# Loading two experts' input weights in 8 KB rows, with tokens gathered in the matching channel order

## The chip, the cores and the metric

The program runs on one core of a Trainium2 chip. The metric is the device time of one execution in microseconds (us); the runs of the kernel before took 2385.02, 2388.09 and 2391.01 us, a median of 2388.09. A core has a matrix engine (PE, whose weight loads are shown as PEld), a vector engine (DVE), a scalar engine (ACT), a GpSimd engine (POOL) and a sync engine (SP). Here SP issues nearly all transfers from HBM, and 16 DMA engines carry them.

## The reference

One layer of a hybrid backbone works on 512 latent tokens and 256 context tokens of 2048 channels: modulated norm, one input projection, three branches (convolution, neighbourhood attention, a gated recurrence), an output projection with a gated residual, and then a mixture of 32 experts, which is where the change lies. Everything is float32.

```
h  = modulated RMSNorm of the residual stream         # 512 x 2048
pg = softmax(h @ w_rg);  grp = argmax                 # one of 4 groups
le = (h @ w_re) of that group; the two best of 8 experts, weights p_exp
for each expert e and its tokens x:
    y = (silu(x @ w1[e]) * (x @ w3[e])) @ w2[e]       # 2048 -> 512 -> 2048
out = residual + gate * sum of the weighted y;  final RMSNorm
```

For each expert `w1` and `w3` are 2048 x 512 and `w2` is 512 x 2048, 4 MB each. The 32 experts' weights are 403 MB in all, out of 589 MB that the kernel reads.

## The kernel before, in words

The order of all instructions is written by hand; engines run their own queues in that order. The input projection takes the first half, then comes the output projection (until about 1300 us), the routing of tokens (to about 1312 us), and the experts, two at a time, in 16 passes that I number as pairs 0 to 15.

Each expert has 64 slots for tokens. A pair uses the two halves of PE's columns: expert `e` in columns 0 to 63, `e + 1` in 64 to 127, so two matmuls run side by side. For the products with `w1` and `w3` (`expert_pair`, matmul at L1359) the gathered tokens `hs[k]` (128 channels by 256 slots) are the stationary side, and the weights of the same 128 channels (128 x 512) are the moving side; 16 contraction steps `k` are summed. Then come the activation (L1370, L1386), a transpose (L1391), the product with `w2` in four runs of 512 columns (`down`, L1403), the scaling by slot weights (`scaled`, L1410), a split into high and low parts (L124, L125) and a product with a one-hot matrix that returns the slots to their tokens (`combine`, L1338), which DVE adds to the residual (L1340).

Weights come in tiles of 1 MB. `add` (L1034) cuts `w1` and `w3` so that one tile holds two contraction steps of both experts: partition p holds channel 128 k + p, so each piece that a partition receives is one weight row of 512 floats, 2 KB. `load_weights` (L1059) issues two transfers of 512 KB for a tile, one for each expert, as far ahead as there are places: six in a pool of their own (`NW`), one in the experts' pool, and eight former homes of other data, of which five are given back during the first two pairs (`until`). Ten stay. `next_w` (L1076) hands out the next tile when its first matmul is written, and returns the place of the one before it. A tile lasts four of the paired matmuls. There are 24 tiles to a pair: 8 of `w1`, 8 of `w3`, 8 of `w2`.

Four experts' tokens are gathered at a time by products with a one-hot matrix (`gather`, L1267). It has 16 steps: four runs of 512 channels, for each four blocks of 128 tokens. For a step, `token_parts` (L1139) makes the high part of 128 tokens by 512 channels on ACT (L1149, a cast) and the low part on DVE (L1150, a subtraction), and eight matmuls (L1291) follow. Two steps' parts are kept at a time, so a step's parts are made after the matmuls of the step two before it. After each fourth step DVE scales four channel tiles with the modulation `A2` and the norm (L1307), and ACT adds `B2` (L1308). The gather for the next four experts goes on beside the odd pairs: three steps each beside the first two quarters of `w3`, two each beside the others, one after them, four beside the `w2` products, and one in the next pair (`STEPS`). The first gather comes before and beside pair 0; its first three low parts are made on POOL, beside the routing on DVE.

During the output projection `constant` (L1012) works out the constant part of the router's logits on DVE and PE, in ticks 14 and 15 of 64.

Of the kernel before, what the change touches and what calls it, by code (L numbers as in the profile page):

```python
# [8 lines left out]
F32 = mybir.dt.float32  # L9
# [3 lines left out]
AF = mybir.ActivationFunctionType  # L13
# [19 lines left out]
NSTART = 6                      # units of the input projection that go on beside the start  # L33
LEAD = 2
SUMS = (3, 6, 9)                # steps of a modulation run at which the sums of the run before go on
BUDGET, ATTN, MOST = 0.7, 1.0, 3  # what a tick has room for on the vector engine
NW = 6                          # weight tiles in their own pool
# [9 lines left out]
def hybrid_block_kernel(ctx: ExitStack, tc: tile.TileContext, I, out):  # L47
# [13 lines left out]
    # ---------------------------------------------------------------- constants  # L61
# [21 lines left out]
    sel = vec[:, 300:302]           # rows 32 g + {0, 1}  # L83
    strips = vec[:, 302:306]        # rows 32 g
    sc = work.tile([P, KT, 2], F32, name="sc")
    nc.scalar.activation(sc, c_in, AF.Silu)
    mods = const.tile([P, 6, KT, 2], F32, name="mods")   # A1, B1 of both streams; ga1, B2, A2, ga2
    warm = const.tile([P, 1], F32, name="warm")

    def table(f):  # L90
        """has the scalar engine's table ready before it is needed"""
        nc.scalar.activation(warm, ones[:, 0:1], f)
# [3 lines left out]
    def rsqrt_newton(dst, v, r):  # L96
        """one Newton step from r towards dst = v ** -0.5; v is lost"""
# [4 lines left out]
    # ------------------------------------------------------------------ tiles  # L102
# [25 lines left out]
    # ------------------------------------------------------------------ start: norm and modulation  # L128
    cs = work.tile([P, KT, 32], F32, name="cs", tag="bias", bufs=2)   # zero-padded stationaries
# [9 lines left out]
    # weights in the order of their use: of the modulation, and of the first units  # L139
# [59 lines left out]
    def modulated(k):  # L199
        """the modulated tokens of a channel tile, in two parts"""  # L200
# [5 lines left out]
    def product(po, h, l, mh_, ml_, first, last):  # L206
        """high x high, high x low and low x high parts"""
# [26 lines left out]
    # three steps for a channel tile: its modulation's rows; its tokens; its products  # L234
# [23 lines left out]
    def context():  # L258
        """its norm and modulation"""
# [38 lines left out]
    # ------------------------------------------------- masks  # L298
# [11 lines left out]
    # ------------------------------------------------- work that goes on beside the projections  # L310
    mix = {}
    taps = deque()        # single instructions of the depthwise convolution
    stages = deque()      # generators of the branches, run one after the other
    mod_ops = deque()

    def step(n=1):
        """the next steps of the branches; returns what they leave for the end of the tick"""
# [14 lines left out]
    # ---- the rest of the modulation: weighted rows summed on the vector engine, partitions on the tensor engine  # L332
# [53 lines left out]
    # ---- convolution module, channel-major  # L386
# [55 lines left out]
    # ---- gated linear recurrence, channel-major, chunks of 128  # L442
# [14 lines left out]
    def context_key(d, fc, kc):  # L457
        """context keys, each decayed to the end of the context, in place of the decays' tile"""
# [23 lines left out]
    def hgrn(h, z, vals, q, g):  # L482
        iv, ivc = vals
        near = (1, 0)                                     # half of a block that holds t; the other holds s
        pp = [z[0][0], z[1][0]]                           # decay from the start of its block to a query
        ks = [z[0][1], z[1][1]]
        st = [t2("st0"), t2("st1")]                       # decay from a key to the end of its block
# [30 lines left out]
        def products(b, keys, queries, other=0):  # L518
            """of keys with queries of the same half of a chunk, or of the other one"""
# [120 lines left out]
    def by_unit(t):  # L640
        """natural token order seen as (column unit of 8, row, column)"""
        return t.rearrange("p (r u c) -> p u r c", r=ROWS, c=8)
# [1029 lines left out]
```

## Time and profile before

| what | value |
|---|---|
| median of three runs | 2388.09 us (2385.02 to 2391.01) |
| profiled execution: span, first to last instruction | 2378.7 us |
| what lies around the span (median less span) | 9.4 us |
| PE busy | 2248.1 us, 95% |
| DVE, ACT, POOL busy | 1259.8, 692.0, 268.8 us |
| moved by DMA | 600.81 MB, of it 317232 packets on SP's queue |
| packets of 8 KB and more | 162 of 321234 |

The page gives no time of its own for the profiled execution beside its span; the median is 9.4 us above the span, which is taken as constant. A busy time of PE includes the modelled ends of matmuls, so a PE that is busy 95% of the time may still be waiting a little in each matmul: start times are the better measure, and most readings below use them. In rows of a timeline the first number is the start in us from the span's start, the second how long the merged instructions took, then engine, line, operation, what is written and read, shape and count, and in brackets the idle time before and what ended it.

### The profile page before, as it was taken

The page shows a single profiled execution, that of the slowest core. Times are in us where ns is not written, and L with a number is a line of the kernel's source. Part 1 is how long each engine was busy: PE and PEld are TensorE (multiplying, and loading weights), DVE is VectorE, ACT ScalarE, POOL GpSimd, SP SyncE. Part 2 cuts the span into 40 slices and gives each one's busy share as a digit, 9 for nine tenths or more (in the row PEclk, how much of TensorE's full clock was granted, in tenths as well). Part 3 has the DMA queues.
Part 4 walks back from the last instruction along what each step waited for, and adds up shares of the span by engine and source line. Part 5 has one row for each costly group of instructions (what it writes and reads, how often), then busy time and mean ns, then how long its engine had stood idle before and what let it go on. Part 6 is the DMA issues. An engine that isn't in the chain of part 4 may idle for free. (4 is left out here: it accounts for less than half of the span.)

```text
span 2378.7 us, 32438 instructions
## 1 busy us (share of the span) xinstructions
PE 2248.1 (95%) x12145; PEld 1416.7 (60%) x12145; DVE 1259.8 (53%) x2204; ACT 692.0 (29%) x1382; POOL 268.8 (11%) x320
## 2 busy tenths in 40 slices
PE   6998999989899999999999999999999999999996
PEld 2456877778777878787777544444534444444433
DVE  4348898898876666434323344443524333434424
ACT  4235223323244453445343321121203121211202
POOL 0006133152421111212000000000000000000000
PEclk9999999999899999999999999999999999999998
DMA  8875434434464555322645799999999999999997
GB/s 304 275 254 170 133 104 132 140 99 135 148 184 150 160 164 158 105 70 63 208 140 199 245 361 336 387 386 387 386 386 386 387 386 386 386 384 387 384 387 264
DMA packets 321234, 600.81 MB, mean 253 GB/s; under 512 B 25392, under 2 KB 35376, under 8 KB 321072
## 3 DMA queue, kind: packets, MB, share of 16 engines
q1 hardware_dynamic: 317232, 593.44, 71.8%
q0 software_dynamic: 3840, 5.25, 1.0%
q8 instruction: 97, 1.59, 0.3%
q14 instruction: 65, 0.53, 0.1%
HBM read 589.15 MB, written 4.19 MB: 249 GB/s over the span
## 5 line engine op out<-in xcount | busy, mean ns | idle before, releaser
L210 PE MATMUL p<-xh,wl 128*128 128x512 f32 (+1 forms) x1184 | 421.2, 356 | 39.1 <-DVE wl L125 35.6
L208 PE MATMUL p<-xh,wh 128*128 128x512 f32 (+1 forms) x1184 | 434.0, 367 | 2.6 <-ACT wh L124 2.2
L1359 PE MATMUL held<-w,hg 128*64 128x512 f32 x1848 | 428.7, 597 | 3.7 <-DMA w<-w 3.0
L209 PE MATMUL p<-xl,wh 128*128 128x512 f32 (+1 forms) x1184 | 418.4, 353 | 0.0
L1359 PEld LDWEIGHTS held<-w,hg 128*64 128x64 f32 x1848 | 129.8, 136 | 251.1 <-issue 211.2
L125 DVE TENSOR_TENSOR wl<-w,wh 128x512 fp32r<-128x512 f32 x216 | 173.7, 804 | 197.6 <-ACT wh L124 192.7
L210 PEld LDWEIGHTS p<-xh,wl 128*128 128x128 f32 x1184 | 225.0, 190 | 83.9 <-DVE wl L125 48.1
L208 PEld LDWEIGHTS p<-xh,wh 128*128 128x128 f32 x1184 | 225.2, 190 | 43.2 <-issue 8.0
L209 PEld LDWEIGHTS p<-xl,wh 128*128 128x128 f32 x1184 | 225.4, 190 | 31.7 <-issue 1.4
L124 ACT CAST wh<-w 128x512 fp32r<-128x512 f32 x216 | 133.8, 620 | 375.4 <-PE p L209 286.6
L1403 PE MATMUL held<-w,at 128*64 128x512 f32 (+1 forms) x944 | 211.9, 591 | 10.9 <-ACT at L1393 10.9
L351 DVE SCALAR_TENSOR_TENSOR m_acc<-w_ada,sc,m_acc 128x512 f32<-128x512 f32 x240 | 213.2, 889 | 13.8 <-DMA w_ada<-w_ada 10.5
L1340 DVE TENSOR_TENSOR xf<-pc,xf 128x512 f32<-128x512 f32 (+1 forms) x244 | 149.6, 675 | 50.6 <-PE pc L1338 50.5
L1150 DVE TENSOR_TENSOR parts<-xr,parts 128x512 fp32r<-128x512 f32 x112 | 76.9, 692 | 170.7 <-ACT parts L1149 170.7
L1291 PEld LDWEIGHTS held<-oh,parts 128*128 128x128 f32 x896 | 112.2, 188 | 66.9 <-issue 46.9
L1291 PE MATMUL held<-oh,parts 128*128 128x256 f32 x896 | 129.3, 290 | 14.2 <-ACT hg L1308 10.3
L1403 PEld LDWEIGHTS held<-w,at 128*64 128x64 f32 x944 | 62.7, 136 | 127.2 <-issue 107.8
L1149 ACT CAST parts<-xr 128x512 fp32r<-128x512 f32 x112 | 68.7, 620 | 170.2 <-PE held L1291 169.4
L124 ACT CAST wh<-ys 128x512 fp32r<-128x512 f32 x60 | 37.2, 620 | 255.2 <-DVE ys L1410 147.7
L1338 PE MATMUL pc<-wh,oht 128*128 128x512 f32 (+1 forms) x260 | 105.8, 408 | 0.0
L208 PE MATMUL po<-mx,wh 128*128 128x512 f32 x256 | 103.0, 402 | 1.1 <-ACT mx L977 0.7
L1338 PE MATMUL pc<-wl,oht 128*128 128x512 f32 (+1 forms) x260 | 101.7, 392 | 0.1
(349 smaller groups left out, 2852.9 us busy)
## 6 DMA issues: line engine op xcount, KB each, us to landing
w<-w SPq DMA_DIRECT2D x692, 512.0 KB
w_ada<-w_ada SPq DMA_DIRECT2D x384, 256.0 KB
w<-w_in SPq DMA_DIRECT2D x184, 256.0 KB
wm<-w SPq DMA_DIRECT2D x74, 512.0 KB
w<-w_out SPq DMA_DIRECT2D x64, 256.0 KB
w_st<-w_st SPq DMA_DIRECT2D x32, 192.0 KB
x<-xT SPq DMA_DIRECT2D x16, 256.0 KB
xt<-xT SPq DMA_DIRECT2D x16, 256.0 KB
```

The costliest lines, as they stand in the source:

```text
L124: nc.scalar.copy(wh, w)
L125: nc.vector.tensor_sub(wl, w, wh.bitcast(F32))
L208: nc.tensor.matmul(po, h, mh_, start=first, stop=False)
L209: nc.tensor.matmul(po, h, ml_, start=False, stop=False)
L210: nc.tensor.matmul(po, l, mh_, start=False, stop=last)
L351: nc.vector.scalar_tensor_tensor(accs[j], loads.popleft(), sc[:, kt, 0:1], accs[j], op0=ALU.mult, op1=ALU.add)
L1150: engine.tensor_tensor(l, x_, h.bitcast(F32), op=ALU.subtract)
L1291: nc.tensor.matmul(pg[i], y[:, cc(i)], oh[:, t], start=t == 0 and m == 0 and i % 2 == 0, stop=t == 3 and m == 1 and i % 2 == 1)
L1338: nc.tensor.matmul(pc[:, 0:n], oht[:, cc(t)], y[:, 0:n], start=m == 0, stop=m == 1)
L1340: nc.vector.tensor_tensor(x_, pc[:, 0:n], x[:, t, o:o + n], op=ALU.add)
L1359: nc.tensor.matmul(acc[64 * j:64 * j + 64], hs[k][:, sl + 64 * j:sl + 64 * j + 64], w[:, j, k % 2], start=k == 0, stop=k == KT - 1, tile_p ...
L1403: nc.tensor.matmul(pd[64 * j:64 * j + 64, 0:n], at[:, 128 * f + 64 * j:128 * f + 64 * j + 64], w[:, j, f - f0], start=f == 0, stop=f == 3, ...
```

## The change: what it does

`w1` and `w3` are cut another way. A tile holds one expert's 512 channels 512 c to 512 c + 511, and partition p gets the four neighbouring channels 512 c + 4 p + i, i = 0 to 3. These are 8 KB in one run of HBM. One transfer of 1 MB brings a tile. A quarter `c` of the contraction now takes two tiles at once, one of each expert, which `next_w(2)` hands out together. `w2` is left as it was.

A contraction step must then have tokens' channels 512 c + 4 q + i on partition q. `token_parts` reads the residual in that order, every fourth float, and writes the parts contiguously as before. The modulation vectors `A2` and `B2` are needed in the same order (`mod2`): 16 small matmuls with every fourth column of the identity, and one copy, do that in tick 15 of the output projection. Comments are taken out of the file as well, which moves line numbers only.

```diff
+    mod2 = const.tile([P, 2, KT], F32, name="mod2")
...
             nc.vector.tensor_tensor(cl, pcn[:, 0:NL], br, op=ALU.add)
+            pq = bank("pq")
+            for m in range(4):
+                for i in range(4):
+                    nc.tensor.matmul(pq[32 * m:32 * m + 32, 0:2 * KT].rearrange("p (w g i) -> p w g i", w=2, i=4)[:, :, :, i],
+                                     ident[:, i::4], mods[:, 3:5, m::4, 0], start=True, stop=True, tile_position=(0, 32 * m))
+            nc.vector.tensor_copy(mod2, pq[:, 0:2 * KT].rearrange("p (w k) -> p w k", w=2))
...
+    def add_run(name, e, c):
+        wseq.append((0, 0, I[name][e, 512 * c:512 * c + 512].rearrange("(p k) n -> p k n", p=P)))
...
-            for k in range(0, KT, 2):
-                add(name, e, k, 2, 0, 512)
+            for c in range(4):
+                for j in range(2):
+                    add_run(name, e + j, c)
...
-                w = rows(w, nk, c)
-                for j in range(2):
-                    nc.sync.dma_start(w[:, j], v[:, j])
+                if nk:
+                    w = rows(w, nk, c)
+                    for j in range(2):
+                        nc.sync.dma_start(w[:, j], v[:, j])
+                else:
+                    nc.sync.dma_start(w, v)
...
-        x_ = xr[:, t, 512 * c:512 * c + 512]
+        x_ = xr[:, t, 512 * c:512 * c + 512].rearrange("p (q i) -> p i q", i=4)
...
-        nc.scalar.copy(h, x_)
-        engine.tensor_tensor(l, x_, h.bitcast(F32), op=ALU.subtract)
+        h4, l4 = (y.rearrange("p (i q) -> p i q", i=4) for y in (h, l))
+        nc.scalar.copy(h4, x_)
+        engine.tensor_tensor(l4, x_, h4.bitcast(F32), op=ALU.subtract)
...
-                    nc.vector.scalar_tensor_tensor(h, pg[i], A2[:, k:k + 1], norm, op0=ALU.mult, op1=ALU.mult)
-                    nc.scalar.activation(h, h, AF.Identity, bias=B2[:, k:k + 1])
+                    nc.vector.scalar_tensor_tensor(h, pg[i], mod2[:, 1, k:k + 1], norm, op0=ALU.mult, op1=ALU.mult)
+                    nc.scalar.activation(h, h, AF.Identity, bias=mod2[:, 0, k:k + 1])
...
+                ws = next_w(2)
                 for k in range(4 * c, 4 * c + 4):
-                    if k % 2 == 0:
-                        w = next_w()
                     for j in range(2):
-                        nc.tensor.matmul(acc[64 * j:64 * j + 64], hs[k][:, sl + 64 * j:sl + 64 * j + 64], w[:, j, k % 2],
+                        nc.tensor.matmul(acc[64 * j:64 * j + 64], hs[k][:, sl + 64 * j:sl + 64 * j + 64], ws[j][:, k % 4],
                                          start=k == 0, stop=k == KT - 1, tile_position=(0, 64 * j))
```

## Rows read from the trace of the kernel before

**Rows 1.** The page: its first line, and what the DMA engines moved in each of 40 equal slices of the span (59.5 us each).

```profile
span 2378.7 us, 32438 instructions
...
GB/s 304 275 254 170 133 104 132 140 99 135 148 184 150 160 164 158 105 70 63 208 140 199 245 361 336 387 386 387 386 386 386 387 386 386 386 384 387 384 387 264
```

**Rows 2.** The table by stretches, for 1500 to 2300 us: stretch, its length, then busy time (and count) of PE, PEld, DVE, ACT and POOL, PE's granted clock, the DMA engines' mean busy share, GB/s.

```profile
1500.00:2300.00 800.00, 770.51 (x3727) 356.47 (x3725) 325.82 (x586) 147.39 (x273) 0.00 (x0) 1.00 1.05 386
```

**Rows 3.** Who waited for whom, from 1319 to 2352 us: who, for whom, us in total, times, longest.

```profile
PEld held L1359 <- DMA w<-w: 32.8, 71, 1.2
```

**Rows 4.** PE's timeline: the matmuls of L1376, which stand between a pair's `w1` and `w3` products, of the odd pairs 1, 3, 5, 7, 9, 11, 13 and 15.

```profile
1398.33 0.86 PE L1376 MATMUL pa<-aux,oh 128*128 128x33 f32 x6
...
1526.83 0.74 PE L1376 MATMUL pa<-aux,oh 128*128 128x33 f32 x5
...
1655.67 0.74 PE L1376 MATMUL pa<-aux,oh 128*128 128x33 f32 x5
...
1787.11 0.74 PE L1376 MATMUL pa<-aux,oh 128*128 128x33 f32 x5
...
1917.07 0.74 PE L1376 MATMUL pa<-aux,oh 128*128 128x33 f32 x5
...
2048.62 0.86 PE L1376 MATMUL pa<-aux,oh 128*128 128x33 f32 x6
...
2179.98 0.74 PE L1376 MATMUL pa<-aux,oh 128*128 128x33 f32 x5
...
2309.84 0.86 PE L1376 MATMUL pa<-aux,oh 128*128 128x33 f32 x6
```

**Rows 5.** PE's timeline: L1376 of pair 14 and the transposes L1391 that follow its `w3` products; a stretch of the `w3` products of pair 15, and the transposes that follow them.

```profile
2255.65 0.74 PE L1376 MATMUL pa<-aux,oh 128*128 128x33 f32 x5
...
2271.48 0.65 PE L1391 MATMUL pt<-cf,act 128*128 128x128 f32 x4 [0.86 <-DVE act L1386]
...
2318.82 2.43 PE L1359 MATMUL held<-w,hg 128*64 128x512 f32 x8 [0.28 <-DMA w<-w]
...
2332.45 0.65 PE L1391 MATMUL pt<-cf,act 128*128 128x128 f32 x4 [0.86 <-DVE act L1386]
```

**Rows 6.** The DMA view, SP's queue: packets, MB, and the time that they took as a share of 16 engines' time; first for 1500 to 2300 us (weights, packets of 2 KB), then for 2371 to 2378.7 us (the last stores of the output, in packets of 4 KB).

```profile
q1 hardware_dynamic: 159884, 308.22, 104.4%
...
q1 hardware_dynamic: 578, 2.10, 67.7%
```

**Rows 7.** The timeline of the gather beside pair 7: its step 2 (first three rows), steps 10 and 11 up to the transposes L1391 (next five), and the `w2` products' first quarter (last four).

```profile
1793.65 0.62 ACT L1149 CAST parts<-xr 128x512 fp32r<-128x512 f32 x1 [4.82 <-PE held L1291]
1794.31 0.69 DVE L1150 TENSOR_TENSOR parts<-xr,parts 128x512 fp32r<-128x512 f32 x1 [2.65 <-ACT parts L1149]
...
1795.05 1.10 PE L1291 MATMUL held<-oh,parts 128*128 128x256 f32 x7 [0.26 <-DVE parts L1150]
...
1816.81 0.62 ACT L1149 CAST parts<-xr 128x512 fp32r<-128x512 f32 x1 [1.29 <-PE held L1291]
1817.47 0.69 DVE L1150 TENSOR_TENSOR parts<-xr,parts 128x512 fp32r<-128x512 f32 x1 [2.52 <-ACT parts L1149]
1817.76 0.62 ACT L1149 CAST parts<-xr 128x512 fp32r<-128x512 f32 x1 [0.33 <-PE held L1291]
...
1819.02 0.68 DVE L1386 TENSOR_TENSOR act<-held,act 128x512 f32<-128x512 f32 x1
...
1819.76 0.66 PE L1391 MATMUL pt<-cf,act 128*128 128x128 f32 x4 [0.45 <-DVE act L1386]
...
1825.81 0.62 ACT L1149 CAST parts<-xr 128x512 fp32r<-128x512 f32 x1 [4.78 <-PE held L1291]
...
1827.08 1.65 DVE L1307 SCALAR_TENSOR_TENSOR hg<-held,mods,norm 128x256 f32<-128x256 f32 x4
...
1828.64 0.74 DVE L1410 SCALAR_TENSOR_TENSOR ys<-held,tw,ga2b 128x512 f32<-128x512 f32 x1
...
1830.82 0.50 PE L1338 MATMUL pc<-wl,oht 128*128 128x512 f32 x1
```

**Rows 8.** DVE's timeline: the reduction L1014, which reads 576 floats at a step of 144 bytes; a reduction of 128 neighbouring floats (L1197); two products of 256 floats each at a step of 8 bytes (L501). Then, from the view of line L1271, products of 256 floats of which one side is read in order: shortest, median and longest time in ns.

```profile
1146.43 1.20 DVE L1014 TENSOR_REDUCE ws<-wr 128x36 f32<-128x576 f32 x1
...
1303.72 0.29 DVE L1197 TENSOR_REDUCE me<-lg 128x16 f32<-128x128 f32 x1
...
285.55 0.76 DVE L501 TENSOR_TENSOR qq<-hq,f 128x256 f32<-128x256 f32 x2
...
L1271 DVE TENSOR_TENSOR oh<-iota,place x32: 415/419/426, 1311.5 to 2182.5; 128x256 fp32r<-128x256 f32 x32
```

**Rows 9.** The timeline of the routing: POOL's three low parts, and two of DVE's instructions beside them.

```profile
1304.23 2.64 POOL L1150 TENSOR_TENSOR wl<-xr,wh 128x512 fp32r<-128x512 f32 x2 [48.33 <-ACT wh L1149]
...
1304.45 1.28 DVE L1203 SCALAR_TENSOR_TENSOR w<-lg,rev 128x144 f32<-128x144 f32 x1
...
1306.81 1.32 POOL L1150 TENSOR_TENSOR part<-xr,part 128x512 fp32r<-128x512 f32 x1
1306.94 1.23 DVE L1209 TENSOR_TENSOR gh<-w,gm 128x16 f32<-128x16 f32 x1
```

**Rows 10.** PE's timeline in the input projection: a small product of four columns (two records to a matmul), and the matmul after it.

```profile
681.18 0.28 PE L364 MATMUL pm<-vec,rows 128*128 128x4 f32 x2
681.32 0.48 PE L208 MATMUL p<-xh,wh 128*128 128x512 f32 x1
```

More of the change, by code (lines that the diff above doesn't have):

```diff
@@ L1070, in load_weights, with next_w @@
                     w = four(at, "w")
-                w = rows(w, nk, c)
-                for j in range(2):
-                    nc.sync.dma_start(w[:, j], v[:, j])
+                if nk:
[4 more added lines that the diff above has]
+                    nc.sync.dma_start(w, v)
                 wtiles.append((w, at))
-    def next_w():
+    def next_w(n=1):
         places.extend(used)
@@ L1080, in next_w @@
         load_weights()
-        w, at = wtiles.popleft()
-        used.append(at)
-        return w
+        ws = []
+        for _ in range(n):
+            w, at = wtiles.popleft()
+            used.append(at)
+            ws.append(w)
+        return ws if n > 1 else ws[0]
     def beside_out(i, n):
```

## The prediction

> **What bounds the kernel now.** I read the page first, to see which stages are full of what [rows 1]: transfers run far below their best for most of the kernel, and at 384 to 387 GB/s without a dip from about 1490 us to 2320 us. That is the experts' stage, the only one whose loads change. The table by stretches says that both candidates are full there: PE busy 770.5 of 800 us at its full granted clock, DMA engines at 1.05, 386 GB/s [rows 2]. So busy shares do not tell which of the two sets the end, and I went to the waits [rows 3]: PE's weight loads for the `w1` and `w3` products waited 32.8 us for weights, in 71 waits. Part of this overlaps running matmuls, so I measured the loss by start times.
>
> The matmuls of L1376 stand at the same place of each odd pair; from one to the next lies the same work, four experts [rows 4]. The seven distances are 128.50, 128.84, 131.44, 129.96, 131.55, 131.36 and 129.86 us. The shortest is PE's own pace; the excess of the others over it is 0.34 + 2.94 + 1.46 + 3.05 + 2.86 + 1.36 = 12.0 us. After the last of them come the `w3` products of pair 15: 2332.45 - 2309.84 = 22.61 us, where those of pair 14, with the same work, took 2271.48 - 2255.65 = 15.83; the bracket in between names the wait for `w` [rows 5]. That is 6.8 us more. The transfers' own pace explains it: a tile of 1 MB at 386 GB/s takes 2.72 us, 48 tiles 130.4 us, against 128.5 us for PE. The stage is bound by transfers by a hair: 12.0 + 6.8 = 18.8 us in all is what PE loses to them, and no speed of loading can win more.
>
> **The change part by part.**
>
> *The packets.* In 1500 to 2300 us SP's queue took 1.044 x 16 x 800 = 13,363 us of engine time for 308.22 MB, 88.8 ns for 2 KB; at the end, in 4 KB packets, 0.677 x 16 x 7.7 = 83.4 us for 2.10 MB, 163 ns for 4 KB, that is 81 ns for 2 KB [rows 6]. Those are stores, and the trace has no bulk load in larger packets, so the gain has two ends: nothing, or, when a part per packet (88.8 + 88.8 - 163 = 15 ns) is paid once instead of four times, 12% of the time of `w1` and `w3`. I take what the 4 KB row itself shows, 8%: 2.49 us a tile. A loss from larger packets is excluded by nothing but this row. What decides is only whether transfers fall below PE's pace: 32 x + 16 x 2.72 = 128.5 gives x = 2.66 us, so 2% is enough. At 2.49 the four experts take 123.2 us and the 18.8 us go.
>
> *Two tiles at a time.* A quarter now needs two tiles before its second matmul and returns them together, 3.44 us later. Of ten places two are in use, eight hold a lead. The greatest demand is the end: from L1376 of pair 14 to the end of `w3` of pair 15, 54.2 + 15.8 = 70 us [rows 4, 5], 32 tiles that arrive in 24 x 2.49 + 8 x 2.72 = 81.5 us: 11.5 us short, 4.6 tiles of eight. It fits, so I cost this at nothing while transfers are quicker; if they are not, each of the last quarters starts up to a tile later, and the cover is gone (rival 2). SP issues 256 fewer transfers; it has nothing else to do here.
>
> *Tokens read at a step of 16 bytes.* `token_parts` reads as many floats as before, so a gain is excluded. DVE at a step of 8 bytes shows no price: two instructions of 256 floats in 0.76 us, where in-order ones take 0.42 each. At 144 bytes it shows one: L1014 took 1.20 us for 576 floats, and from 0.29 us for 128 and 1.05 ns a float ((0.69 - 0.42) us over 256, L1150 against L1271) it would be 0.76 [rows 7, 8]. The excess is 0.76 ns a float, 0.39 us for 512. Sixteen bytes lies between, much nearer to 8; but the two rows differ in that at 144 bytes no two floats lie together, and at 16 bytes with runs of one the reads are of that sort too. I take 0.39 us on DVE (ends 0 and 0.39). ACT shows no such read; its ends are the same, and I take the middle, 0.2.
>
> Where it is paid [rows 7]: at step 2 PE waits already for the parts, made 0.62 + 0.69 us after the step before the last; the chain grows by 0.59 and PE with it. At steps 10 and 11, DVE's second low part now ends near 1819.8 and L1386, queued behind it, near 1820.5 instead of 1819.70; the transposes wait for it: 0.8 us. In the first `w2` quarter L1307 and L1410 stand behind the part on DVE, and the split and the return to tokens, with no room left at 1830.82, behind them: 0.59. The other steps' parts are ready microseconds ahead. Together 2.0 us per gather, seven gathers: 13.9 us (9.7 with a free ACT, 17.9 with 0.39 there, 0 with both free).
>
> *The first gather.* POOL's three low parts take 1.3 us each, and DVE's products in the routing do not end before them: L1203 took 1.28 us and L1209 1.23 for 144 and 16 floats [rows 9]. The routing leads to the first matmul of the experts, so what POOL loses, PE loses: 0 to 3 x 0.39 = 1.2 us by DVE's price; I take 1.2. [...]
>
> *`mod2`.* Sixteen small matmuls on PE in the output projection, where PE is the bound, so nothing hides them. A product of four columns takes PE 681.32 - 681.18 = 0.14 us until the next can start [rows 10]: 2.2 us. Ends: 0.6, if four of them overlap in the four column groups, and 2.2 plus a wait for a bank, some 3. DVE's copy lies beside matmuls.
>
> **Sum.** -18.8 + 13.9 + 1.2 + 2.2 = -1.5 us on the profiled span of 2378.7; with the 9.4 us around it, 2386.6, say 2387 us, against the median 2388.09.
>
> **Rivals.**
>
> 1. *The step of 16 bytes is free, as that of 8 is.* Then only `mod2` is paid: -18.8 + 2.2 = -16.6, 2371 us. For it: the row nearest in bytes shows no price. Against: that row's floats lie two to 16 bytes, these one. [...]
>
> 2. *The stage stays bound by its transfers,* because the rows are still sent in pieces of 2 KB, or the pace is set behind the packets. It decides from 2.66 us a tile up. Then the 18.8 us stay; PE's new pace, 128.5 + 2.0 to 2.6, lies 0.1 to 0.7 us above the transfers' 130.4, up to 4.6 us over seven distances; the last quarter has four matmuls left when its second tile lands instead of two, 0.9 us; and 1.2 + 2.2 are paid: +9, 2397 us, slower. For it: 386 GB/s is steady like a ceiling. Against: the 4 KB row is above that ceiling.
>
> 3. *Strided reads cost more:* ACT pays 0.39 us and POOL the most, or delays pile up in DVE's queue, which has little room in a `w2` quarter with L1307. [...]
>
> **How the numbers follow.** Forecast 0.40, rival 1 0.36, rival 2 0.12, rival 3 0.12. A measurement of this kernel tells from no change about 0.3%, 7.2 us: 2381 to 2395. The forecast's own range is 2380 to 2393 (the ends of ACT's price and of `mod2`). The whole range takes in rivals 1 and 2: 2368 to 2398. Faster by over 0.3%: rival 1 and 0.04 of the forecast, 0.40. Slower: rival 2 mostly, part of rival 3 and a little of the forecast, 0.18. Within: 0.42.
>
> **What would show it.** Transfers: packets of 8 KB on SP's queue, distances of L1376 all alike, `w3` of pair 15 at about 15.8 us, no waits for `w`, and GB/s that dips between pairs; wrong if distances still vary and rates stay flat. Stride: L1150 at 1.08 us and L1149 at 0.8; distances of 130.5 us; if both are unchanged, distances of 128.5 and rival 1. Routing: POOL at 1.7 us each. `mod2`: about 2 us more in tick 15. The forecast is wrong if the distances fall to 128.5 (faster) or the waits for weights stay (slower).

## The result, and the profile after

The change made the kernel slower: a median of 2406.30 us over four runs (2401.42 to 2409.64) against 2388.78 us over four runs of the kernel before (2385.02 to 2391.01), a ratio of 1.0078, 95% interval 1.0061 to 1.0095. Forecast were 2387 us and a range of 2368 to 2398. The profiled execution has a span of 2399.5 us, 20.8 us more than before [rows 1], and a time of 2401.42 us.

Lines of the page after; the last two are the groups of `token_parts` on DVE and ACT (busy us, mean ns of one, idle before).

```profile
span 2399.5 us, 32240 instructions
...
GB/s 305 277 253 163 132 110 124 137 101 136 151 176 149 160 165 160 97 68 58 214 144 185 257 341 327 408 363 400 359 388 394 354 407 352 409 358 408 363 400 262
...
L1170 DVE TENSOR_TENSOR parts<-xr,parts 128x512 fp32r<-128x512 f32 x112 | 119.7, 1089 | 159.7 <-ACT parts L1169 159.7
...
L1169 ACT CAST parts<-xr 128x512 fp32r<-128x512 f32 x112 | 122.5, 1124 | 138.0 <-PE held L1311 131.0
```

DVE's part grew from 0.69 to 1.09 us, ACT's from 0.62 to 1.12 [rows 7]. The steady 386 GB/s has become an up and down, 350 to 409. The waits of SP's queue from 1319 to 2352 us (who, for whom, us, times, longest) tell why; three rows of the change, then the longest of the kernel before:

```profile
SPq L1089 <- PE held L1378: 226.6, 55, 13.2
SPq L1089 <- PE held L1422: 209.9, 89, 7.9
SPq L1087 <- DMA w<-w: 128.6, 137, 2.1
...
SPq L1073 <- DMA w<-w: 411.7, 555, 2.5
```

SP issues the next tile when PE has given back a place; transfers are quicker than PE and wait for it. Before, SP waited mostly for transfers. The DMA view shows how quick; first while `w1` and `w3` load, then while `w2` does.

```profile
DMA packets 1497, 10.92 MB, mean 420 GB/s; under 512 B 165, under 2 KB 165, under 8 KB 165
...
q1 hardware_dynamic: 1496, 10.90, 101.2%
...
DMA packets 3993, 7.72 MB, mean 386 GB/s; under 512 B 230, under 2 KB 230, under 8 KB 3992
```

Packets of 8 KB move 420 GB/s, those of 2 KB 386 as before: a tile of 1.049 MB takes 2.50 us, against the 2.49 forecast. The loading did what it should. PE's timeline, the matmuls between `w1` and `w3` of the odd pairs (they answer to [rows 4]):

```profile
1408.39 0.86 PE L1395 MATMUL pa<-aux,oh 128*128 128x33 f32 x6
...
1539.96 0.86 PE L1395 MATMUL pa<-aux,oh 128*128 128x33 f32 x6
...
1671.42 0.74 PE L1395 MATMUL pa<-aux,oh 128*128 128x33 f32 x5
...
1804.58 0.86 PE L1395 MATMUL pa<-aux,oh 128*128 128x33 f32 x6
...
1937.91 0.86 PE L1395 MATMUL pa<-aux,oh 128*128 128x33 f32 x6
...
2069.74 0.86 PE L1395 MATMUL pa<-aux,oh 128*128 128x33 f32 x6
...
2201.31 0.86 PE L1395 MATMUL pa<-aux,oh 128*128 128x33 f32 x6
...
2332.76 0.97 PE L1395 MATMUL pa<-aux,oh 128*128 128x33 f32 x7
```

The distances are 131.57, 131.46, 133.16, 133.33, 131.83, 131.57 and 131.45 us. Nearly all are alike, as forecast for a stage that no longer waits for weights, but at 131.5 and not at 130.5: PE's own four experts grew by 3.0 us, from 128.5. Two stick out by 1.7 to 1.9. PE's timeline of the gather beside pair 7, from the parts of step 11 to the second `w2` quarter, then the start of the `w2` products of pair 9, and last two rows of the kernel before beside pair 7, which go with the transposes at 1819.76 in [rows 7]:

```profile
1835.86 0.38 PE L1311 MATMUL held<-oh,parts 128*128 128x256 f32 x1 [0.19 <-ACT parts L1169]
1836.96 1.09 PE L1311 MATMUL held<-oh,parts 128*128 128x256 f32 x7 [0.72 <-DVE parts L1170]
1838.57 0.66 PE L1410 MATMUL pt<-cf,act 128*128 128x128 f32 x4 [0.51 <-DVE act L1405]
1839.90 5.19 PE L1422 MATMUL held<-w,at 128*64 128x512 f32 x16 [0.68 <-ACT at L1412]
...
1851.36 0.50 PE L1358 MATMUL pc<-wh,oht 128*128 128x512 f32 x1 [0.40 <-ACT wh L125]
1852.09 0.50 PE L1358 MATMUL pc<-wl,oht 128*128 128x512 f32 x1 [0.23 <-DVE wl L126]
...
1973.32 3.65 PE L1422 MATMUL held<-w,at 128*64 128x512 f32 x16 [0.68 <-ACT at L1412]
...
1818.21 1.10 PE L1291 MATMUL held<-oh,parts 128*128 128x256 f32 x7 [0.31 <-DVE parts L1150]
...
1821.09 3.65 PE L1403 MATMUL held<-w,at 128*64 128x512 f32 x16 [0.67 <-ACT at L1393]
```

Read the brackets: PE waits for the parts (0.19 + 0.72), for L1405 behind them on DVE (0.51), for ACT's copy (0.68), and in the first `w2` quarter for the split (0.40 + 0.23). Three of these waits stood there before, shorter or as long: 0.31 for the parts, 0.45 for L1386 and 0.67 for the copy. The new ones lie where the prediction put them, but most of what it put before the transposes falls on the parts of step 11, just ahead of them. Then the fourth row: sixteen matmuls in 5.19 us, where pair 9 and the kernel before have them in 3.65. The table by stretches says why (columns as in [rows 2], the granted clock is the third number from the end):

```profile
1839.90:1845.00 5.10, 5.10 (x16) 1.42 (x16) 0.30 (x1) 0.00 (x0) 0.00 (x0) 0.69 1.03 421
```

The granted clock was 0.69 there: it was 0.50 until 1843.0 us and 1.00 behind, after PE had stood still four times, 2.1 us in all, within 4.2 us (before: three times, 1.4 us, and no fall in any of the seven gathers). It fell in pairs 5 and 7, and in none of the other gathers of this execution. The waits for weights did not all go either; PE's `w3` products of pair 15:

```profile
2338.69 3.65 PE L1378 MATMUL held<-w,hg 128*64 128x512 f32 x16 [0.41 <-DMA w<-w]
2343.68 3.65 PE L1378 MATMUL held<-w,hg 128*64 128x512 f32 x16 [1.34 <-DMA w<-w]
2348.71 3.65 PE L1378 MATMUL held<-w,hg 128*64 128x512 f32 x14 [1.38 <-DMA w<-w]
```

The transposes behind them start at 2353.21 us, so this stage took 2353.21 - 2332.76 = 20.45 us, where 15.8 were forecast and 22.61 stood before [rows 5]. Ahead of the experts, two edits can be read directly: `mod2` (L1024), and POOL's low parts beside DVE in the routing (they answer to [rows 9]).

```profile
1153.14 1.45 PE L1024 MATMUL pq<-mods,cf 128*32 128x8 f32 x32
1154.52 0.50 PE L209 MATMUL po<-mx,wh 128*128 128x512 f32 x1
...
1311.65 3.06 POOL L1170 TENSOR_TENSOR wl<-xr,wh 128x512 fp32r<-128x512 f32 x2 [48.49 <-ACT wh L1169]
...
1314.66 1.65 POOL L1170 TENSOR_TENSOR part<-xr,part 128x512 fp32r<-128x512 f32 x1
```

`mod2` holds PE for 1154.52 - 1153.14 = 1.4 us. POOL's parts take 1.53 and 1.65 us instead of 1.32.

### The profile page after: what moved, and what is told of

Its sections match the earlier page's. It is cut to its first block, busy times and chain, and to the rows that moved or that the text cites. A ratio compares the mean times of both kernels' runs of the same rounds, so it can differ in the third digit from the quotient of the medians.

```text
span 2399.5 us, 32240 instructions
## 1 busy us (share of the span) xinstructions
PE 2253.1 (94%) x12177; PEld 1421.5 (59%) x12177; DVE 1307.2 (54%) x2205; ACT 752.4 (31%) x1382; POOL 270.2 (11%) x320
## 5 line engine op out<-in xcount | busy, mean ns | idle before, releaser
L1378 PE MATMUL held<-w,hg 128*64 128x512 f32 x1848 | 457.1, 596 | 4.6 <-DMA w<-w 3.1
L1378 PEld LDWEIGHTS held<-w,hg 128*64 128x64 f32 x1848 | 141.6, 137 | 265.7 <-issue 246.2
L1170 DVE TENSOR_TENSOR parts<-xr,parts 128x512 fp32r<-128x512 f32 x112 | 119.7, 1089 | 159.7 <-ACT parts L1169 159.7
L1169 ACT CAST parts<-xr 128x512 fp32r<-128x512 f32 x112 | 122.5, 1124 | 138.0 <-PE held L1311 131.0
L1311 PE MATMUL held<-oh,parts 128*128 128x256 f32 x896 | 133.4, 293 | 22.6 <-ACT hg L1328 10.3
```

The lines of the kernel that those rows point to most:

```text
L1169: nc.scalar.copy(h4, x_)
L1311: nc.tensor.matmul(pg[i], y[:, cc(i)], oh[:, t], start=t == 0 and m == 0 and i % 2 == 0, stop=t == 3 and m == 1 and i % 2 == 1)
L1378: nc.tensor.matmul(acc[64 * j:64 * j + 64], hs[k][:, sl + 64 * j:sl + 64 * j + 64], ws[j][:, k % 4], start=k == 0, stop=k == KT - 1, tile_ ...
```

## The experiments

Eleven kernels ran, in three groups, each with runs of the kernel before beside it (medians 2385.4, 2387.1 and 2386.1 us). The table gives what was measured; stages are read from PE's start times, in one profiled execution of each. "Distance" is the mean of the seven distances. "Odd w3" is the stretch from the matmuls between `w1` and `w3` to the transposes, in those of the odd pairs 1 to 13 that do not wait for weights. "Odd w2" is the stretch from the first `w2` product to the next pair's first `w1` product in these pairs, shortest and longest. The last column is the `w3` stretch of pair 15. All in us.

| kernel | median | ratio to before (95%) | distance | odd w3 | odd w2 | w3 of pair 15 |
|---|---|---|---|---|---|---|
| before | 2388.8 | | 130.2 | 31.85 | 24.7 | 22.6 |
| the change | 2406.3 | 1.0078 (1.0061 to 1.0095) | 132.1 | 33.70 | 25.8 to 27.5 | 20.5 |
| rows_only | 2374.3 | 0.9955 (0.9943 to 0.9968) | 128.6 | 31.85 | 24.7 | 20.3 |
| stride_only | 2405.8 | 1.0082 (1.0068 to 1.0097) | 133.1 | 33.70 | 27.3 to 27.5 | 21.5 |
| pe_step | 2481.9 | 1.0410 (1.0396 to 1.0423) | 141.7 | 40.3 to 41.6 | 28.1 | 20.4 |
| two | 2375.9 | 0.9959 (0.9943 to 0.9974) | 128.6 | 31.95 | 24.7 | 18.4 |
| fill | 2398.6 | 1.0048 (1.0035 to 1.0061) | 131.7 | 33.7 | 25.8 to 25.9 | 20.5 |
| stride_fill | 2393.0 | 1.0036 (1.0023 to 1.0049) | 131.4 | 33.7 | 25.8 | 21.4 |
| act_write | 2400.9 | 1.0063 (1.0051 to 1.0075) | 132.8 | 33.7 | 25.7 to 28.8 | 20.7 |
| act_step | 2385.9 | 1.0002 (0.9993 to 1.0010) | 130.4 | 32.9 | 25.2 to 26.9 | 20.3 |
| shift | 2376.4 | 0.9961 (0.9949 to 0.9974) | 128.6 | 31.9 | 24.7 | 20.9 |
| two_pad | 2371.8 | 0.9939 (0.9925 to 0.9954) | 128.5 | 31.93 | 24.7 | 18.5 |
| rows_nw5 | 2390.1 | 1.0013 (1.0003 to 1.0023) | 130.8 | 32.2 | 24.7 | 20.8 |

**The rows alone (rows_only).**

```diff
-        x_ = xr[:, t, 512 * c:512 * c + 512].rearrange("p (q i) -> p i q", i=4)
+        x_ = xr[:, t, 512 * c:512 * c + 512]
...
-                    nc.vector.scalar_tensor_tensor(h, pg[i], mod2[:, 1, k:k + 1], norm, op0=ALU.mult, op1=ALU.mult)
+                    nc.vector.scalar_tensor_tensor(h, pg[i], A2[:, k:k + 1], norm, op0=ALU.mult, op1=ALU.mult)
```

> The changed kernel with its tokens read in order again (token_parts as before) and without mod2: the 8 KB rows and the two tiles at a time are all that is left of the change. The weights' channels then meet other channels of the tokens, so the experts' products are of permuted channels; the work is the same. Theory A (what the two traces suggest: the rows win some 14 us of PE's waits, and the reads at a step of 16 bytes cost 3.0 us per gather): ACT's and DVE's parts back at 0.62 and 0.69 us, distances of the pa matmuls all near 128.5 us, w3 of pair 15 near 20 us, 2372 to 2377 us. Theory B (8 KB transfers or two tiles at a time cost time of their own, and the waits that went did so only because PE itself had become slower): distances of 130 us or more, 2386 us or more.

Measured: 2374.3 us. PE's timeline, the matmuls between `w1` and `w3` of pairs 1 and 15:

```profile
1402.08 0.63 PE L1387 MATMUL pa<-aux,oh 128*128 128x33 f32 x4
...
2302.02 0.74 PE L1387 MATMUL pa<-aux,oh 128*128 128x33 f32 x5
```

Seven distances in 899.94 us, 128.56 each: PE's own pace, and 11.6 us less than before. Theory B falls: 8 KB rows and two tiles at a time win time when nothing else is changed. So all of the loss lies in what the rows need of the tokens and of the modulation (`mod2`).

**The step alone (stride_only).**

```diff
-        x_ = xr[:, t, 512 * c:512 * c + 512]
+        x_ = xr[:, t, 512 * c:512 * c + 512].rearrange("p (q i) -> p i q", i=4)
```

(on the kernel before, with the same edit of the writes as in the change)

> The kernel before with token_parts reading every fourth float, and nothing else: weights in 2 KB rows, one tile at a time, no mod2. The tokens' channels then stand in another order than the weights'; the work is the same. Theory A: parts at 1.12 us (ACT) and 1.09 us (DVE), 3.0 us per gather on PE, so that its own four experts take 131.5 us, just above the transfers' 130.4; nearly all waits for weights between the pa matmuls go, distances of 131.4 to 131.8 against a mean of 130.2 before: 7 x 1.3 = 9, and 2 us for the first gather, less some 3 us of the waits in pair 15: 2396 to 2399 us. Theory B: reads at a step are dearer in the changed kernel because 8 KB rows land beside them; here parts take less than 1.0 us, 2388 to 2392 us.

Measured: 2405.8 us, as slow as the whole change, and 7 to 10 us above theory A's figure. Parts took 1.13 and 1.09 us with rows of 2 KB landing beside them, so theory B falls. What theory A missed stands in the `w2` stages, all seven of 27.3 to 27.5 us instead of 25.8. PE's timeline before and at the start of one of them:

```profile
1969.46 1.10 PE L1292 MATMUL held<-oh,parts 128*128 128x256 f32 x7 [0.72 <-DVE parts L1151]
1971.08 0.66 PE L1392 MATMUL pt<-cf,act 128*128 128x128 f32 x4 [0.53 <-DVE act L1387]
1972.41 5.34 PE L1404 MATMUL held<-w,at 128*64 128x512 f32 x16 [0.68 <-ACT at L1394]
```

and the table by stretches there:

```profile
1969.00:1971.60 2.60, 1.62 (x11) 1.31 (x11) 2.02 (x3) 1.44 (x2) 0.00 (x0) 1.00 1.05 385
1971.60:1975.00 3.40, 2.73 (x8) 0.77 (x8) 1.07 (x1) 0.58 (x1) 0.00 (x0) 0.62 1.05 387
```

The granted clock falls right behind the waits, from 1.00 to a mean of 0.62, and sixteen matmuls take 1.7 us longer. What two gathers showed in the change, seven show here. That became theory C, tried below.

**The step on PE's side (pe_step).**

```diff
-                    nc.tensor.matmul(pg[i], y[:, cc(i)], oh[:, t], start=t == 0 and m == 0 and i % 2 == 0,
+                    nc.tensor.matmul(pg[i], y[:, i::4], oh[:, t], start=t == 0 and m == 0 and i % 2 == 0,
```

(and `token_parts` as before the change)

> The changed kernel, with the step moved from ACT and DVE to PE's weight load: token_parts reads and writes in order as before, and the gather's matmuls take every fourth column of a part as their stationary side. It computes the reference. Theory A, with weight loads that pay nothing for a step of 16 bytes: weight load 0.19 us as before, distances near 128.5, and mod2's 1.4 us beside the rows-only kernel: 2374 to 2379 us, faster than both kernels. If the weight load pays for the step as ACT does (0.19 to about 0.34 us each, 128 of them in a gather, only partly under matmuls): up to 128 x 0.15 x 8 = 150 us more, 2450 us and above.

Measured: 2481.9 us. The gather's weight loads and matmuls in the view of their line (shortest, median and longest ns), and the same in the kernel before:

```profile
L1310 PEld LDWEIGHTS held<-oh,parts x896: 307/329/339, 1424.5 to 2347.3; 128*128 128x128 f32 x180
L1310 PE MATMUL held<-oh,parts x896: 282/396/514, 1424.5 to 2347.4; 128*128 128x256 f32 x180
...
L1291 PEld LDWEIGHTS held<-oh,parts x896: 186/188/191, 1402.9 to 2244.9; 128*128 128x128 f32 x180
L1291 PE MATMUL held<-oh,parts x896: 274/281/390, 1402.9 to 2245.0; 128*128 128x256 f32 x180
```

A load whose columns lie 16 bytes apart takes 329 ns where one in order takes 188, and the short matmuls of the gather do not cover it: their median is 396 ns instead of 281. The second branch of the expectation holds: this is the dearest place for the step.

**Two neighbours instead of four (two).**

```diff
-        x_ = xr[:, t, 512 * c:512 * c + 512].rearrange("p (q i) -> p i q", i=4)
+        x_ = xr[:, t, 512 * c:512 * c + 512].rearrange("p (b q i) -> p b i q", b=2, i=2)
...
-        wseq.append((0, 0, I[name][e, 512 * c:512 * c + 512].rearrange("(p k) n -> p k n", p=P)))
+        wseq.append((0, 0, I[name][e:e + 2, 256 * c:256 * c + 256].rearrange("e (p k) n -> p e k n", p=P)))
...
-                ws = next_w(2)
                 for k in range(4 * c, 4 * c + 4):
+                    if k % 2 == 0:
+                        w = next_w()
```

> Two neighbouring channels per partition instead of four: rows of 4 KB, a tile of 1 MB again holds two contraction steps of both experts and is handed out alone, token_parts reads at a step of 8 bytes, mod2 in that order with 4 matmuls instead of 16. It computes the reference. Theory A: a step of 8 bytes is free on DVE as in the kernel before's own rows, and on ACT too, so parts at 0.62 and 0.69 us; packets of 4 KB take 163 ns, 2.60 us a tile, which is under PE's pace (128.5 us against 32 x 2.60 + 16 x 2.72 = 126.7); one more tile of lead than with two at a time: distances near 128.5, w3 of pair 15 under 20 us, 2373 to 2378 us. Rival: 8 bytes costs half of what 16 do (0.2 us each on ACT and DVE): 1.5 us per gather, distances of 130, 2384 to 2388 us.

Measured: 2375.9 us. The view of ACT's line:

```profile
L1170 ACT CAST parts<-xr x112: 637/656/681, 1409.3 to 2229.9; 128x512 fp32r<-128x512 f32 x112
```

A step of 8 bytes costs ACT 0.04 us and DVE nothing (0.693 us). Distances are those of rows_only, and `w3` of pair 15 waits 1.9 us less, though its packets of 4 KB load more slowly (407 GB/s at 1790 to 1810 us). One tile less held in use would explain it; the kernel differs in more than that, so this is not shown by itself.

**Filling PE's waits (fill, stride_fill).**

```diff
         pt = bank("pt")
+        if ahead:
+            for f in range(4):
+                nc.tensor.transpose(pt[:, cc(f)], ident, ident)
...
             pd = prod()
+            if ahead and c == 0:
+                for f in range(4):
+                    nc.tensor.transpose(pd[:, cc(f)], ident, ident)
```

On the changed kernel:

> The changed kernel with eight transposes of the identity added on PE in each odd pair: four before the real transposes, while PE waits for DVE, and four into the next accumulator's bank before the w2 products, while PE waits for ACT; the real work overwrites both. Theory C (the strided reads lengthen PE's waits between w3 and w2, and where PE has stood for some 2 us in all there the granted clock falls to the lower level at the start of the w2 products, about 1.7 us each time): with the waits filled no w2 stage takes more than 25.9 us, and 3 to 5 falls fewer than in the median run of the change, 2398 to 2402 us. Rival (the falls have nothing to do with PE's waits there): w2 stages of 27 us go on, and 2406 us or a little more for the added work.

On the stride-only kernel:

> The stride-only kernel with the same eight transposes of the identity added in each odd pair (its tokens' channels stand in another order than the weights', as there). There all seven w2 stages took 27.3 to 27.5 us. Theory C: they come down to about 25.8 us, 7 x 1.6 = 11 us less, part of it given back to waits for weights: 2394 to 2399 us. Rival: they stay at 27.4 and the time at 2405 to 2408 us.

Measured: 2398.6 and 2393.0 us, 0.30% and 0.46% less by the ratios than without the transposes, 7 and 11 us (each give or take 0.2%); the second is 1 us below theory C's range. No `w2` stage is above 25.9 us in either. PE's timeline of stride_fill at the same place as above:

```profile
1961.43 1.10 PE L1292 MATMUL held<-oh,parts 128*128 128x256 f32 x7 [0.72 <-DVE parts L1151]
1962.37 0.60 PE L1393 MATMUL pt<-cf 128*128 128x128 f32 x4
1963.05 0.66 PE L1395 MATMUL pt<-cf,act 128*128 128x128 f32 x4
1963.55 0.60 PE L1404 MATMUL held<-cf 128*128 128x128 f32 x4
1964.39 1.94 PE L1410 MATMUL held<-w,at 128*64 128x512 f32 x8 [0.24 <-ACT at L1397]
```

and its table by stretches right behind, at the full granted clock:

```profile
1965.00:1968.00 3.00, 3.00 (x17) 0.76 (x13) 0.00 (x0) 0.00 (x0) 0.00 (x0) 1.00 1.05 388
```

The real work comes no earlier (from the parts' matmuls to the first `w2` product 2.96 us, 2.95 without), but the clock stays at 1.00 where it was 0.62: here it was the bare stand of PE that let it fall. Theory C holds. stride_fill shows one more thing: with rows of 2 KB its distances are 131.4 us, those of the change without falls. Once PE is that slow, the faster rows win nothing between the pairs.

**Parts of the step (act_write, act_step).** ACT reads in order and writes 512 bytes apart:

```diff
-        nc.scalar.copy(h4, x_)
+        nc.scalar.copy(h.rearrange("p (i q) -> p q i", i=4), xr[:, t, 512 * c:512 * c + 512].rearrange("p (q i) -> p q i", i=4))
```

> The changed kernel, with ACT reading the tokens in order and writing the high part at a step of 512 bytes into the same places; DVE still reads at a step of 16 bytes. It computes the reference. If a write at a step is free on ACT, its parts take 0.62 us again and only DVE's 0.40 us is left: the chain of steps 2, 10 and 11 and the first w2 quarter grow by 0.4 each instead of 0.9, near 1.2 to 1.6 us per gather, and PE's waits are shorter, so that the granted clock falls less often: 2384 to 2392 us. If ACT pays for the write as for the read: 2404 to 2408 us.

ACT's line in that kernel:

```profile
L1169 ACT CAST parts<-xr x112: 1074/1113/1149, 1409.8 to 2259.9; 128x512 fp32r<-128x512 f32 x112
```

The write costs as much as the read did; the first branch falls, and stages are those of the change, with three falls of the clock, of 2.8 to 3.0 us here. Its 2400.9 us lie below the 2404 to 2408 expected of the second. The second kernel takes DVE's step away instead:

```diff
-        engine.tensor_tensor(l4, x_, h4.bitcast(F32), op=ALU.subtract)
+        engine.tensor_tensor(l, xr[:, t, 512 * c:512 * c + 512], h.bitcast(F32), op=ALU.subtract)
```

> The changed kernel with only ACT reading at a step of 16 bytes; DVE reads the tokens and the high part in order, so that the low parts belong to other channels. ACT alone pays, 0.50 us a part: 1.2 to 1.8 us per gather if the two prices add up along the chain of parts, 2384 to 2392 us. If DVE's queue is what sets the loss and ACT's is covered: less than 0.7 us per gather, 2377 to 2382 us. If ACT's is the whole: 3 us per gather, 2398 us and above.

Measured: 2385.9 us. `w3` grew by 1.1 and `w2` by 0.5: 1.6 us per gather for ACT's 0.50 alone, as expected of prices that add up along the chain. DVE's share would then be what is left to 3.0, 1.4; no kernel ran with DVE's step alone. One `w2` stage here has a fall of the clock (26.9 us), behind waits of 1.7 us in all.

**The place of the tiles (shift, two_pad).** In every profile with `mod2`, matmuls of the output projection followed each other more slowly (233.4 ns against 229.1), before `mod2`'s own as well. On rows_only, and on two:

```diff
-    warm = const.tile([P, 1], F32, name="warm")
+    warm = const.tile([P, 33], F32, name="warm")[:, 0:1]
```

```diff
-    mod2 = const.tile([P, 2, KT], F32, name="mod2")
+    mod2 = const.tile([P, 64], F32, name="mod2")[:, 0:2 * KT].rearrange("p (w k) -> p w k", w=2)
```

> The rows-only kernel with 128 bytes per partition of unused room added behind the small constants (where mod2 stands in the changed kernel), and no other edit: no instruction is added, all tiles behind are moved by 128 bytes. (Experts' products are of permuted channels, as in the rows-only kernel.) In the output projection of all five profiled kernels that have mod2 one matmul follows the other after 233.4 ns, in the four without it after 229.1 ns. Theory D (the place of the tiles sets this): 233 ns here too, 2.6 us more between tick 15 and the routing (154.4 instead of 151.8 us), 2376 to 2378 us. Rival (it comes with mod2's instructions): 229 ns, 151.8 us, 2374 us.

> The kernel with two neighbouring channels per partition, with mod2 given 256 bytes per partition instead of 128 (only the first 128 are used). It computes the reference. Theory D with a pattern that repeats within 256 bytes: 229 ns a matmul in the output projection, 2.6 us less between tick 15 and the routing, 2372 to 2374 us, the fastest kernel here. If the pattern is longer than 256 bytes or mod2's instructions are the cause: 233 ns and 2375 to 2377 us.

PE's timeline in shift, two matmuls of the output projection that are 15 apart:

```profile
1157.95 0.39 PE L210 MATMUL po<-mx,wl 128*128 128x512 f32 x1
...
1161.45 0.40 PE L210 MATMUL po<-mx,wl 128*128 128x512 f32 x1
```

and in rows_only, which differs from it by 128 bytes of unused room alone:

```profile
1158.25 0.39 PE L210 MATMUL po<-mx,wl 128*128 128x512 f32 x1
...
1161.68 0.39 PE L210 MATMUL po<-mx,wl 128*128 128x512 f32 x1
```

3.50 / 15 = 233 ns against 3.43 / 15 = 229. From tick 15's product to the routing's first, PE took 154.4 us in shift and 151.8 in rows_only: 2.6 us for the place of the tiles alone; the two medians are too close to tell it (0.9961 and 0.9955). With 256 bytes (two_pad) it is 229 ns again. The stretch is then 153.7 us against 155.0 in two, 1.2 us less where 2.6 were expected; around one wait of PE for ACT, which two does not have, four matmuls take 1.83 us instead of 0.92, and some 0.5 us stay open. That kernel has the lowest median here, 0.6% under the kernel before, but not clear of those of two, rows_only and shift; it leaves out nothing of the work.

**A place less (rows_nw5).**

```diff
-NW = 6
+NW = 5
```

(on rows_only)

> The rows-only kernel with one place less for weights (five in the pool instead of six; nine of 1 MB in the steady state instead of ten, two of them in use). Theory E (the last pair waits because the lead of eight tiles is too small for the two pairs that follow each other at 54 us each, and with two tiles at a time one place less is in the lead): one tile of 2.5 us less lead, w3 of pair 15 from 20.3 to 22.5 to 23 us, and the odd pairs, whose weights came only 2 us ahead at the start of w3, wait 0.5 to 1 us each: 2379 to 2384 us. Rival (the waits are set by the rate of the transfers alone): w3 of pair 15 at 20.3 us and 2374 us.

Measured: 2390.1 us, 14 us (by the ratios) to 16 (by the medians) more than rows_only and beyond what theory E gave. Pair 15 lost 2.1 us in `w1` and 0.5 in `w3`, as expected in sum; but the six odd pairs 3 to 13 lost 2.2 to 2.5 us each in `w1` and `w3`, not 0.5 to 1. The rival falls: it is the lead, counted in places, that keeps PE from waiting here, not the rate alone.

## Why the prediction was wrong, step by step

It got the parts of the change right and the size of three of them wrong (the waits that go, the strided parts, `mod2`), and it left out two effects of which the trace before had no row (a fall of the clock behind these waits, and the place of the tiles) and the parts made during pair 0. The profiled change against rows_only (30.8 us between the spans) divides like this: 7 x 2.99 = 20.9 for strided parts, 3.2 for two falls of the clock, 4.0 for `mod2` and the moved tiles, 1.1 in pair 0, 0.3 for waits for weights, and 0.6 each ahead of tick 15's product and between the logits' last product and the experts' first. The last two are no price of the change: the second of these stretches took 19.5, 20.8 and 23.8 us in shift, rows_only and rows_nw5, which have the same code there, and 19.8 and 22.5 in stride_fill and stride_only.

By the medians the change cost 17.5 us where -1.5 were forecast. Of these 19 us, the parts are 7.0 (20.9 for 13.9), the waits that stayed 4.9, the tiles and `mod2` 1.8 (4.0 for 2.2), pair 0 1.1 and the clock 3.2 in the profile: 18.0, if POOL's 1.2 is left as it was forecast.

- *The packets:* right, 2.50 us a tile against 2.49, and in part by luck. The 8% were read from a row of stores in 4 KB packets; loads in 4 KB packets move 407 GB/s (two), 2.58 us a tile, and it took 8 KB to come to 2.50. Rival 2 is out.
- *The waits go, and two tiles at a time cost nothing:* wrong by 4.9 us. Of 18.8 us that were to go, rows_only won 11.6 between the pairs and 2.3 in pair 15. The sum for the end asked whether 11.5 us fit into a lead of eight tiles, 20 us, taken as full. By the times of the packets in rows_only, the lead was 14.2 us at the first `w3` product of pair 14, and the 30 tiles behind took 81.9 us instead of 22 x 2.50 + 8 x 2.72 = 76.8, since some still waited for places. A tile less of lead cost pair 15 some 2.6 us in rows_nw5. The kernel two, with one tile in use, still took 18.4 us there where 15.8 were forecast, so two tiles at a time are at most a part of it.
- *Tokens read at a step of 16 bytes:* the step that failed most. DVE was right (0.39 forecast, 0.40 measured). For ACT the middle of two ends was taken, 0.2 us, with no row for it; it is 0.50, above the upper end, which was DVE's price. The places were right, but the sum per gather, 2.0 us, is 3.0: 1.85 in `w3` and 1.15 in the `w2` stage, where 1.4 and 0.59 were put. The parts are a chain, ACT, then DVE, then PE, and act_step shows ACT's share at 1.6 by itself. So the mechanism held and a size failed: with ACT's 0.50 in place of 0.2 the same chain gives, as an estimate, 0.9 in step 2, 0.8 + 0.3 before the transposes and 0.9 in the `w2` quarter, 2.9 us. The parts made during pair 0 were not priced; it took 26.0 us from the experts' first product to the end of `w1` instead of 24.9.
- *What a wait on PE costs:* left out. The new waits were priced as time alone. PE stands four times, 2.1 us, between `w3` and `w2` instead of three times, 1.4, and the granted clock then falls behind them at times, 1.5 to 1.7 us each in the change. The kernel fill puts it at 0.3%, 7 us, in the median run of the change. The granted clocks of whole runs fit that: a mean of 0.988 in the profiled run of the change, 0.981 to 0.985 in its three others, and 0.987 or 0.988 in all five of fill.
- *POOL:* 1.53 to 1.65 us a part for 1.7 forecast, some 1.2 times the 1.32 of before. What PE lost by it, forecast as 1.2, stays open: the stretch from the logits' last product to the gather's first took 11.6 us before and 12.1 after, but 11.7, 13.1 and 13.7 in shift, rows_only and rows_nw5, which have no strided part.
- *`mod2`:* 1.4 us against 2.2, inside the ends. Its tile of 128 bytes was priced at nothing and cost 2.6 us by moving all others.
- *The 9.4 us around the span:* misread. After, time and span of one execution differ by 1.9 us (2401.42 and 2399.5). An execution of the kernel before with that span, 2378.7 us, stands among its runs beside the first group: it took 2380.48 us, the quickest of eleven. So the profiled execution was simply a quick one, and the 9.4 us were mostly spread between executions. It was quick ahead of the experts: tick 15's product starts at 1149.0 us in it and at 1151.7 to 1154.3 in the twelve other profiles, so the 20.8 us between the spans overstate the change, and the 17.5 between the medians are the better figure.
- *The rivals:* rival 1 is out: a step of 16 bytes is not free (DVE 1.09 us instead of 0.69, ACT 1.12 instead of 0.62), though one of 8 nearly is (0.69 and 0.66). Rival 3 named the cause, but it let ACT pay no more than DVE, where 0.50 us stand against 0.40, and had no clock in it. That POOL pays the most no run shows: its three parts took 0.75 us more in all, 0.25 each.

The frame of the sum held: -18.8 and +13.9 may be added as long as transfers stay below PE's pace, and they did; its sizes failed. But it left no room for a wrong size, since PE (128.5 us) and transfers (130.4) stood within 2 us of each other. The faster rows can win at most 1.9 us in each four experts between the pairs. The forecast's 2.0 us on PE would just have taken that back; 3.0 lose all of it and 1.1 more, with either rows, as stride_fill shows.

## What to carry to other kernels

Where two resources stand within a per cent or two of each other, compare a change's gain on one with its price on the other, stage by stage, before adding them up; a layout that is better for the transfers must not be paid for on the engine that is next in line. Price an access pattern on each engine that will do it: DVE's price, read from its own row at 144 bytes, came out right and said nothing of ACT's. Look for the mildest form of the layout: two neighbours per partition (4 KB rows, a step of 8 bytes) won the same distances as four (in order) and cost ACT 0.04 us a part and DVE nothing. Look at the places of tiles and at the granted clock behind a new wait as well, since both moved more here (2.6 us the place, 3.2 us the clock) than `mod2` itself (1.4 us).

## What the runs showed of the hardware

- Reading 512 floats at a step of 16 bytes takes ACT 1.12 us instead of 0.62, DVE 1.09 instead of 0.69 and POOL 1.53 to 1.65 instead of 1.32; at 8 bytes ACT 0.66 and DVE 0.69. ACT's write at a step of 512 bytes takes 1.11 us. A weight load of PE at a step of 16 bytes takes 329 ns instead of 188.
- A move of all tiles behind it by 128 bytes turned 229 ns a matmul into 233 in the output projection, and 256 bytes turned it back. Which operand it is, and what it meets, is open.
- Loads on SP's queue moved 386 GB/s in packets of 2 KB, 407 in packets of 4 KB and 420 in packets of 8 KB.
- Stands of PE within some 4 us were followed by a fall of the granted clock in some gathers (to 0.50 in the change and act_write): 1.4 us in all in none of 7 (before), 1.7 in 1 of 7 (act_step), 2.1 in 3 of 7 (act_write), 2 of 7 (the change) and 7 of 7 (stride_only); filled with idle transposes, in none of 14. The brackets of the last three differ by 0.1 us at most; what decides between them was not tried.
